# Strided slice on one core: a held batch moved from 128 partitions to 32 partitions with four rows each

## Chip, core and metric

The kernel runs on one core of one Trainium2 chip. The metric is device time in microseconds of one execution; lower is better.

## What is computed

```python
def reference(x, start, stop, stride):        # x: [32, 1024, 512] float32
    return x[:, start:stop:stride, :]         # start 0, stop 512, stride 2
```

Of each of the 32 batches every second row of the first 512 is copied: 256 rows of 512 float32 values (2 KB). The result is [32, 256, 512], 16.8 MB. There is no arithmetic, so the whole kernel is a set of DMA transfers. In `x` two chosen rows that follow each other start 4 KB apart and a batch starts 2 MB after the one before it. In `out` rows start 2 KB apart and batches 512 KB apart.

## The kernel before

The rows of a batch are parted by parity: 128 even output rows and 128 odd ones. One half is copied directly, from `x` to `out` in HBM. The other half takes a way through SBUF: it is loaded into the tile `held` and stored from there. `apart(b)` says which parity of batch b goes directly (1 for b = 0, 1, 4, 5 of eight, 0 for b = 2, 3, 6, 7). `two(t, b, step, parity)` makes the access pattern of one parity of the two batches b and b + step, with the 128 rows as its first dimension, the two batches as its second and the 512 values as its third. In `x` the 128 rows of one parity are 8 KB apart, in `out` 4 KB.

The batches are taken in four groups of eight (`EIGHT`). In the first double loop (lines 35 to 40) SP issues four loads in each group, each of two batches that follow each other (line 39), and ACT issues four direct copies, of the pairs (0, 5), (2, 7), (1, 4) and (3, 6) of the group (line 40). `held` is [128, 32, 512]: partition p holds row p of the loaded parity, for all 32 batches. Each transfer is 512 KB and moves rows of 2 KB.

In the second double loop (lines 41 to 47) both queues wait for the loads of a group, which count on a semaphore of their own in the list `loaded`, and then store it: four stores, each of batches b and b + 4, SP taking even b and ACT odd b (line 47). Each queue issues its instructions in the order of the program. ACT comes to its stores once it has issued all direct copies, SP once it has issued all loads. At the end SP waits for all stores and direct copies (lines 48 and 49), by the semaphores `done`. The tile is as large as all that is loaded, so no buffer is used twice.

The order is written out by hand; no scheduler moves a transfer.

Of the kernel before, what the change touches and what calls it, by code (L numbers as in the profile page):

```python
# [3 lines left out]

EIGHT = 8


def apart(b):


    return 1 - (b >> 1 & 1)


def two(t, b, step, parity):

    return t[b : b + step + 1 : step].rearrange("b (p two) d -> two p b d", two=2)[parity]


def kernel(tc, x, start, stop, stride, out):

    nc = tc.nc
    src = x[:, start:stop:stride, :]
    B, rows, D = out.shape
    P = rows // 2
    sp, act = nc.sync, nc.scalar
    groups = range(0, B, EIGHT)
    with tc.tile_pool(name="io", bufs=1) as io:  # L30
        held = io.tile([P, B, D], x.dtype, name="held")
        with tc.tile_critical():
            loaded = [nc.alloc_semaphore(name=f"loaded{g}") for g in groups]
            done = [nc.alloc_semaphore(name=f"done{i}") for i in range(2)]
            for g in groups:
                for i, (b, step) in enumerate(((0, 5), (2, 5), (1, 3), (3, 3))):
                    b += g
                    at = g + 2 * i
                    sp.dma_start(held[:, at : at + 2], two(src, at, 1, 1 - apart(at))).then_inc(loaded[g // EIGHT], 16)
                    act.dma_start(two(out, b, step, apart(b)), two(src, b, step, apart(b))).then_inc(done[1], 16)  # L40
            for g in groups:
                for queue in (sp, act):
                    queue.wait_ge(loaded[g // EIGHT], 16 * 4)
                for b in range(g, g + 4):
                    k = b % 2
                    to = two(out, b, 4, 1 - apart(b))
                    (sp, act)[k].dma_start(to, held[:, b : b + 5 : 4]).then_inc(done[k], 16)
            sp.wait_ge(done[0], 16 * (B // 4))
            sp.wait_ge(done[1], 16 * (B // 2 + B // 4))


# [1 line left out]
_INS = ['x', 'start', 'stop', 'stride']  # L53
_OUTS = [((32, 256, 512), 'float32')]

_NUMBERS = {'start': 0, 'stop': 512, 'stride': 2}


def kernel(**inputs):
    import numpy as _np  # L60
    import concourse.bacc as _bacc
    import concourse.tile as _tile
    from concourse import mybir as _mybir
    from concourse.bass_utils import run_bass_kernel_spmd as _run

    nc = _bacc.Bacc("TRN2", target_bir_lowering=False, num_devices=1)  # L66
    arrays, args = {}, []
    for name in _INS:
        if name in _NUMBERS:
            args.append(_NUMBERS[name])  # L70
            continue
        a = _np.ascontiguousarray(inputs[name])
        if a.dtype.kind in "iu":
            a = a.astype(_np.int64)
        arrays[f"in_{name}_dram"] = a
        args.append(nc.dram_tensor(f"in_{name}_dram", a.shape, _mybir.dt.from_np(a.dtype), kind="ExternalInput").ap())
    for i, (shape, dtype) in enumerate(_OUTS):
        dt = _mybir.dt.from_np(_np.dtype(dtype))
        args.append(nc.dram_tensor(f"out_{i}_dram", shape, dt, kind="ExternalOutput").ap())
    with _tile.TileContext(nc) as tc:  # L80
        kernel(tc, *args)
    r = _run(nc, [arrays], core_ids=[0])
    got = tuple(r.results[0][f"out_{i}_dram"] for i in range(len(_OUTS)))
    return got[0]
```

## Time and profile before

| | |
|---|---|
| median of 13 runs | 80.67 us (80.23 to 81.87) |
| the profiled execution's own time | 81.33 us |
| its span in the profile | 79.5 us |
| packets on the DMA engines | 13,056, of which 12,288 carry 2 KB and 768 signal completion |
| mean rate of the DMA engines over the span | 316 GB/s |
| loads (line 39) | 16 of 512 KB, median 22.6 us from issue to landing |
| direct copies (line 40) | 16 of 512 KB, median 22.6 us |
| stores (line 47) | 8 on SP and 8 on ACT, of 512 KB, median 20.9 and 20.7 us |

The span is the time from the first to the last recorded instruction; the execution's own time has some 1.8 us around it. GB/s counts what the 16 DMA engines of the core carried: a row that goes directly counts once, a row that goes through `held` counts twice, so that 16.8 MB of result are 25.2 MB of transfers. Queue q1 is SP's and q10 is ACT's. Both queues run on the same 16 engines. Time from issue to landing includes the wait behind what was issued before on the same queue.

The page's tables by compute engine hold nothing but four small fills by GpSimd at the start. Besides the page, the trace answers with a table by stretch of time (rate and busy share of the DMA engines), and it holds a record of every packet with its start, duration, queue and size.

### The profile page before, as it was taken

The page shows a single profiled execution, that of the slowest core. Times are in us where ns is not written, and L with a number is a line of the kernel's source. Part 1 is how long each engine was busy: PE and PEld are TensorE (multiplying, and loading weights), DVE is VectorE, ACT ScalarE, POOL GpSimd, SP SyncE. Part 2 cuts the span into 40 slices and gives each one's busy share as a digit, 9 for nine tenths or more (in the row PEclk, how much of TensorE's full clock was granted, in tenths as well). Part 3 has the DMA queues.
Part 4 walks back from the last instruction along what each step waited for, and adds up shares of the span by engine and source line. Part 5 has one row for each costly group of instructions (what it writes and reads, how often), then busy time and mean ns, then how long its engine had stood idle before and what let it go on. Part 6 is the DMA issues. An engine that isn't in the chain of part 4 may idle for free. (4 is left out here: it accounts for less than half of the span.)

```text
span 79.5 us, 99 instructions
## 1 busy us (share of the span) xinstructions
POOL 0.2 (0%) x4
## 2 busy tenths in 40 slices
POOL 0000000000000000000000000000000000000000
DMA  0899999999999999899999999999999999999930
GB/s 0 262 309 284 278 222 363 358 362 382 325 317 367 241 319 397 294 336 357 332 357 352 323 372 272 345 357 409 408 409 356 351 350 350 355 356 354 350 118 4
DMA packets 13056, 25.17 MB, mean 316 GB/s; under 512 B 768, under 2 KB 768, under 8 KB 13056
## 3 DMA queue, kind: packets, MB, share of 16 engines
q10 hardware_dynamic: 6528, 12.58, 47.6%
q1 hardware_dynamic: 6528, 12.58, 47.6%
HBM read 16.78 MB, written 16.78 MB: 422 GB/s over the span
## 5 line engine op out<-in xcount | busy, mean ns | idle before, releaser
L66 POOL MEMSET const-bfloat16-1.0<- 128x1 bf16 x1 | 0.1, 101 | 0.0
L66 POOL MEMSET const-uint8-127<- 128x1 uint8 x1 | 0.1, 101 | 0.0
L66 POOL MEMSET const-float32-0.0<- 128x1 f32 x1 | 0.1, 98 | 0.2 <-issue 0.2
L66 POOL MEMSET const-float32-1.0<- 128x1 f32 x1 | 0.1, 98 | 0.0
## 6 DMA issues: line engine op xcount, KB each, us to landing
out_dram<-in_x_dram ACTq DMA_DIRECT2D x16, 512.0 KB, 22.6
held<-in_x_dram SPq DMA_DIRECT2D x16, 512.0 KB, 22.6
out_dram<-held SPq DMA_DIRECT2D x8, 512.0 KB, 20.9
out_dram<-held ACTq DMA_DIRECT2D x8, 512.0 KB, 20.7
```

Of the source, the lines that this page charges most:

```text
L66: nc = _bacc.Bacc("TRN2", target_bir_lowering=False, num_devices=1)
```

## The change

A batch is now held by 32 partitions, with four rows in each. `held` becomes [128, 8, 4, 512]: batch b lies in the quarter b % 4 of the partitions, 32 x (b % 4) and on, at place b // 4. Its size stays the same, 64 KB in each partition. `place(b, n)` gives the part of the tile that holds n batches, and `pieces(t, b, n, parity)` the rows of one parity of n batches as [32 n, 4, 512].

- A load is of one batch, 256 KB, into 32 partitions; there are 32 instead of 16, in the order 0, 2, 1, 3, 4, 6, 5, 7 in each group, so that quarters 0 and 2 are followed by 1 and 3. A partition takes four rows, which are 8 KB apart in `x`.
- A store is of batches b and b + 1, from 64 partitions, 512 KB. SP stores those with b = 0 and 4 of the group, from partitions 0 to 63, ACT those with b = 2 and 6, from partitions 64 to 127. There are still 8 on each queue.
- A group's semaphore counts eight loads instead of four.
- The direct copies are the same, and stand in the same places on ACT.

In the built program the loads' pattern in `x` is 128 rows 8 KB apart, and the stores' in `out` 256 rows 4 KB apart; the SBUF side is 32 or 64 partitions of four rows of 2 KB. If the 16 engines take runs of equal length of these rows, an engine's part begins 64 KB after its neighbour's, in `x` for loads and in `out` for stores.

```diff
+QUARTER = 32
+DEEP = 4
...
+def pieces(t, b, n, parity):
+
+    rows = t[b] if n == 1 else t[b : b + n].rearrange("b r d -> (b r) d")
+    return rows.rearrange("(p s two) d -> two p s d", s=DEEP, two=2)[parity]
...
-    P = rows // 2
...
-        held = io.tile([P, B, D], x.dtype, name="held")
+        held = io.tile([4 * QUARTER, B // 4, DEEP, D], x.dtype, name="held")
+
+        def place(b, n):
+            first = QUARTER * (b % 4)
+            return held[first : first + n * QUARTER, b // 4]
...
                 for i, (b, step) in enumerate(((0, 5), (2, 5), (1, 3), (3, 3))):
+                    for at in ((0, 2), (1, 3), (4, 6), (5, 7))[i]:
+                        at += g
+                        sp.dma_start(place(at, 1), pieces(src, at, 1, 1 - apart(at))).then_inc(loaded[g // EIGHT], 16)
                     b += g
-                    at = g + 2 * i
-                    sp.dma_start(held[:, at : at + 2], two(src, at, 1, 1 - apart(at))).then_inc(loaded[g // EIGHT], 16)
                     act.dma_start(two(out, b, step, apart(b)), two(src, b, step, apart(b))).then_inc(done[1], 16)
             for g in groups:
                 for queue in (sp, act):
-                    queue.wait_ge(loaded[g // EIGHT], 16 * 4)
-                for b in range(g, g + 4):
-                    k = b % 2
-                    to = two(out, b, 4, 1 - apart(b))
-                    (sp, act)[k].dma_start(to, held[:, b : b + 5 : 4]).then_inc(done[k], 16)
+                    queue.wait_ge(loaded[g // EIGHT], 16 * EIGHT)
+                for b in range(g, g + EIGHT, 2):
+                    k = b // 2 % 2
+                    (sp, act)[k].dma_start(pieces(out, b, 2, 1 - apart(b)), place(b, 2)).then_inc(done[k], 16)
```

## The prediction

> **What bounds the kernel now.** I read the page's slices and queue table first, then the table by stretch of time, then the issue table and the wait list. No compute engine does anything, so the time is that of 12,288 packets of 2 KB on 16 DMA engines, 768 each.
>
> ```profile
> span 79.5 us, 99 instructions
> DMA  0899999999999999899999999999999999999930
> q10 hardware_dynamic: 6528, 12.58, 47.6%
> q1 hardware_dynamic: 6528, 12.58, 47.6%
> HBM read 16.78 MB, written 16.78 MB: 422 GB/s over the span
> ```
>
> The reader is to see that the DMA engines are busy from the second slice to the last but two, and that the queues of SP and ACT get equal shares. A packet sooner is a gain only if it takes an engine less long. How long it takes shows in the rate by stretch:
>
> ```profile
> core 0: us, POOL busy (x), PEclk, DMA share, GB/s
> 2.00:56.00 54.00, 0.00 (x0) 1.00 1.00 330
> 54.00:55.00 1.00, 0.00 (x0) 1.00 1.06 408
> 56.00:57.00 1.00, 0.00 (x0) 1.00 1.06 410
> 56.00:76.00 20.00, 0.00 (x0) 1.00 1.06 361
> 68.00:70.00 2.00, 0.00 (x0) 1.00 1.07 353
> 76.00:79.50 3.50, 0.00 (x0) 1.00 0.10 36
> ```
>
> The last number of a row is GB/s. 16 x 2048 bytes over it is an engine's pace per packet: 99.3 ns up to 56 us, where loads and direct copies run (stage one), 90.8 ns from 56 to 76 us, where stores run (stage two), and 80.3 ns at 54 to 55 us, the best seen. 768 packets at 80.3 ns would be 61.7 us; they took from 2.0 to 77.9 us. The 14 us between: stage one 330 x 54 us = 17.8 MB = 544 packets an engine x 19.0 ns = 10.3 us; stage two 220 packets x 10.5 ns = 2.3 us; a tail from 76 us on, in which few engines still work, some 1.5 us. The trace's packet records tell the nature of the loss: most packets take exactly 84 ns (the next starts 4 ns before the end). In stage one some 316 took over 200 ns, many of them ending within some 50 ns of others, and hold nearly all the excess; in stage two none did, but from 59 us on about half take 86 to 200 ns.
>
> Issue and semaphores are not the limit:
>
> ```profile
> out_dram<-in_x_dram ACTq DMA_DIRECT2D x16, 512.0 KB, 22.6
> held<-in_x_dram SPq DMA_DIRECT2D x16, 512.0 KB, 22.6
> SPq L49 <- DMA out_dram<-held: 19.5, 1, 19.5
> SPq L47 <- DMA held<-in_x_dram: 0.5, 1, 0.5
> ```
>
> A DMA lands 22.6 us after its issue, so the rings hold over 20 us of work, and the one wait of 0.5 us for loads (line 47) hides behind them. SP then waits 19.5 us for stores only at the end.
>
> **What the Trainium skill says.** "DMA: Bandwidth & Descriptors", section "The descriptor swizzle": a transfer over 128 partitions gives engines 0 to 7 partitions 4e to 4e+3 and 32+4e to 35+4e, engines 8 to 15 the upper half. Neighbouring engines of a load would then read x 4 x 8 KB = 32 KB apart, those of a store write 4 x 4 KB = 16 KB apart, each engine with a port of its own. Its section "Why a DMA increments its semaphore by 16 and not by 1" lets 32 or 64 partitions still use 16 engines, since 16 divides both; which engine gets which rows it does not say, and I assume runs of equal length. "SBUF — State Buffer", section "Door 1: The DMA port swizzle", says that partitions 0 to 31 or 0 to 63 reach only 8 of 16 ports, 189 to 196 GB/s at 1 MiB against an asymptote of 218 (27.2 a port). No stretch of this trace shows such a shape. "Latency and other measured facts" on the first page gives copies between HBM tensors 207 GB/s at a row pitch of 512 KB and 214 at best, and less only at pitches of 2 MB and more; the trace can't confirm or deny it, as it varies no pitch.
>
> **The change part by part.**
>
> *16 loads of 512 KB become 32 of 256 KB.* Packets stay 2 KB and 4,096. Each engine has 16 completion packets more, at 9 ns in the packet records: 0.15 us. That they cost more at a boundary is excluded by 53 to 59 us, where completions pass and the rate stays at 399 to 410. SP issues 16 DMAs more, at 433 ns (the least for a load) to 652 ns (the least on ACT) each, 7 to 10 us in all; that runs under the backlog of 20 us and costs nothing except at the start. Two loads go with one direct copy, 1.05 MB or 3.2 us at 330 GB/s; SP needs some 1.9 us for them at 0.94 us each, the longest that an ACT issue took in the first 2 us. Over 1.6 us each the cover would be gone.
>
> *Start.* The first load may be issued in 652 instead of 433 ns: 0 to 0.2 us. Loads run alone from 2.0 to 3.6 us, at some 246 GB/s by the slices of that stretch; over 8 ports at 189 to 218 that is 1.6 us x (1 - 189/246) = 0.4 us at most, 0.2 at least. I take 0.4 for both.
>
> *Loads over 32 partitions.* Two neighbouring engines now share a port. On average the loads bring 330/2 = 165 GB/s, under 189, so a port isn't full. But a load packet can find its partner at work: the port needs 2048/27.2 = 75 ns, the partner puts one there every 199 ns, so 38% of packets wait 37 ns on average, 14 ns x 256 packets = 3.6 us for random phases with no read-ahead; nothing if the pairs fall into opposite phase, which alternating with direct copies permits. I take a sixth, 0.6 us[...].
>
> *Stores over 64 partitions.* SP's stores read partitions 0 to 63, ACT's 64 to 127, so each queue has 8 ports and engines e and e+8 share one. At 361/2 = 180 GB/s a queue stands close to 189. By the same sum: partner every 182 ns, 41% x 37 ns x 256 = 3.9 us at random, 0 at best; I take a sixth, 0.65 us. Where one queue works alone, as at 75 to 76 us where most packets are ACT's, another 0.1 us.
>
> *Distance of the engines, 64 KB in x and in out.* This is the part that the trace does not show, so it is bounded on both sides. For it: load packets stall more often than direct ones (194 against 122 over 200 ns from 2 to 56 us). Against it: the mean of both is 99.2 ns there, and from 20 to 56 us the direct ones, which stand at 64 KB in x already, are the slower. Stalls that end together hit direct copies too, six engines at a time for 1.2 to 1.5 us. For loads all excess gone is (99.2 - 84) x 256 = -3.9 us; a worsening as large is not excluded, +3.9. For stores: -2.3 us (408 GB/s held to the end) to (99.3 - 90.8) x 220 = +1.9 us, if they take on stage one's pace. I take 0 for both.
>
> *Waits and order.* `loaded` counts 128 instead of 64; a group of loads ends at the same byte. Stores take b and b+1 together, needing the same group, and SP and ACT still have 8 each. Behind SP's waits stand only its stores, with 20 us queued ahead. Cost nothing, on that cover.
>
> Sum: 0.15 + 0.4 + 0.6 + 0.65 + 0.1 = +1.9 us. The profiled execution took 81.33 us, 1.8 us around its span of 79.5, so 83.2 us by its own time; it lay 0.66 us above the median of 80.67 us, against which I forecast **82.6 us**.
>
> **Rivals.**
> 1. *Likeliest, 0.40: shared ports nibble, distance does nothing.* 82.6 us, its own range 81 to 84.
> 2. *Slower by more, 0.15: paired engines stay in step,* two thirds of the port waits count: 2.4 + 2.6 + 0.65 = +5.6 us, 86.3. For it: all engines get equal DMAs at once, and stage two has 5 to 21% of room to the port limit (180 against 189 to 218). Against: at the best pace every packet is 84 ns, so engines drift only by stalls, and opposite phase is stable.
> 3. *Faster, 0.39: the distance cures stalls.* One mechanism, 16 streams meeting in one part of HBM. With half of the loads' excess gone (-1.95) and stores at 385 GB/s instead of 361 (-1.25), against 0.65 for start, completions and tail: -2.5 us, 78.1 us. It decides once it saves more than 1.9 us, that is 7.4 ns on each load packet alone. For it: groups of load stalls ending together, and the fall from 408 to 353 GB/s among stores, which neither queue nor port explains. Against: direct copies with that distance are no better.
> 4. *The change doesn't do what it says, or gains and costs cancel, 0.06:* the rows are dealt to engines otherwise, distances stay mixed; 80.7 us.
>
> **How the numbers follow.** Slower is cases 1 and 2, 0.55; faster 0.39; within 0.3% (0.24 us, about what a measurement of this kernel can tell from no change) 0.06. The range 78.0 to 86.2 us takes in case 1, nearly all of case 2 up to its centre, and case 3 down to its centre.
>
> **What would show it.** Right: over the first 54 us the rate stays at 320 to 335 GB/s with as many packets over 200 ns in loads as now; stage two falls to 340 to 352; the 408 GB/s stretch at the turn of the stages gets shorter or lower; the first 2 us of transfer are slower. Wrong: stage one at 345 or more, or stage two near 400, says the distance matters and ports don't; a rate per queue that never passes 190 with packets at 100 ns and more throughout says case 2. A longer gap before the first packet would be issue cost that I put at 0.2 us.

## The result, and the profile after

The changed kernel takes 82.12 us (median of 11 runs, 81.65 to 82.57) against 80.62 us before (48 runs): ratio 1.0175, 95% interval 1.0144 to 1.0206. It is slower by 1.4 to 1.5 us; the forecast was 82.6 us. The sign and the size came out, but the experiments below show that most of the terms of the sum were put in the wrong place.

The two profiled executions lie nearer to each other than the medians: 81.33 us before (0.7 above its median) and 81.72 after (0.4 below). So the profiles show how the two kernels differ in kind, and less than the whole difference in size: their last packets end 0.5 us apart. The page after:

```profile
span 79.9 us, 115 instructions
DMA  0799899999999999999999999999999999999730
q1 hardware_dynamic: 6784, 12.59, 47.2%
q10 hardware_dynamic: 6528, 12.58, 45.8%
HBM read 16.78 MB, written 16.78 MB: 420 GB/s over the span
```

The queue of SP (q1) has 256 packets more than before: 16 loads more, each with 16 completions. Its share of engine time is no larger (47.2% of 79.9 us against 47.6% of 79.5), so a packet did not get dearer on average; ACT's share even fell, from 47.6% to 45.8%. The same stretches as in the prediction, after:

```profile
core 0: us, POOL busy (x), PEclk, DMA share, GB/s
2.00:56.00 54.00, 0.00 (x0) 1.00 0.99 328
56.00:57.00 1.00, 0.00 (x0) 1.00 1.03 399
56.00:76.00 20.00, 0.00 (x0) 1.00 1.02 359
68.00:70.00 2.00, 0.00 (x0) 1.00 1.06 353
76.00:79.90 3.90, 0.00 (x0) 1.00 0.17 67
```

Stage one moves at 328 GB/s (330 before), stage two at 359 (361), and its settled part at 353 in both. What differs is the last row: 67 GB/s over 3.9 us, where before had 36 over 3.5. Neither the loads nor the stores got slower as a whole; the end got longer. A finer table shows it. (The changed kernel's 362 GB/s from 60 to 73 us, below, still holds a part of the fast stretch at the turn of the stages, which comes later in it.) Before:

```profile
60.00:73.00 13.00, 0.00 (x0) 1.00 1.06 353
73.00:75.00 2.00, 0.00 (x0) 1.00 1.07 348
75.00:76.00 1.00, 0.00 (x0) 1.00 0.98 322
76.00:77.00 1.00, 0.00 (x0) 1.00 0.29 102
77.00:79.00 2.00, 0.00 (x0) 1.00 0.03 11
```

After:

```profile
60.00:73.00 13.00, 0.00 (x0) 1.00 1.06 362
73.00:75.00 2.00, 0.00 (x0) 1.00 0.88 311
75.00:76.00 1.00, 0.00 (x0) 1.00 0.60 231
76.00:77.00 1.00, 0.00 (x0) 1.00 0.43 166
77.00:79.00 2.00, 0.00 (x0) 1.00 0.13 48
```

GB/s times us gives what is left at 73 us: 348 x 2 + 322 + 102 + 22 = 1,142 KB before, 311 x 2 + 231 + 166 + 96 = 1,115 KB after. So at 73 us the changed kernel is not behind. But before keeps its engines busy to nearly 76 us (share 1.07, 0.98), and all but one of them then stop within about a microsecond, while after has idle engines from 73 us on (0.88, 0.60, 0.43) and works until 78.4 us. Taken that each engine gets an equal part of every transfer, as the prediction did, the engines run out of equal lists of packets at different times. The packet records, put into chains by their start and end over the last microseconds, give it by engine. This is approximate, to some tenths of a microsecond, since a record doesn't name its engine. Before, 15 of 16 end between 75.7 and 76.8 us and one at 77.9; after, eight end between 76.0 and 78.4 us and eight between some 73 and 75.5. The mean of the 16 is about 76.3 us before and 76.0 after. The time of the kernel is that of its last engine.

The issues and waits, after:

```profile
out_dram<-in_x_dram ACTq DMA_DIRECT2D x16, 512.0 KB, 20.8
held<-in_x_dram SPq DMA_DIRECT2D x32, 256.0 KB, 16.3
SPq L62 <- DMA out_dram<-held: 11.6, 1, 11.6
SPq L60 <- DMA held<-in_x_dram: 0.3, 1, 0.3
```

A load lands 16.3 us after its issue, so once the queues are filled the doubled number of issues hides behind the backlog, as forecast, and the wait for loads is 0.3 us.

### The profile page after: what moved, and what is told of

Same layout as the page of the kernel before. It is cut to its first block, busy times and chain, and to the rows that moved or that the text cites. A ratio compares the mean times of both kernels' runs of the same rounds, so it can differ in the third digit from the quotient of the medians.

```text
span 79.9 us, 115 instructions
## 1 busy us (share of the span) xinstructions
POOL 0.2 (0%) x4
## 3 DMA queue, kind: packets, MB, share of 16 engines
q1 hardware_dynamic: 6784, 12.59, 47.2%
q10 hardware_dynamic: 6528, 12.58, 45.8%
## 6 DMA issues: line engine op xcount, KB each, us to landing
held<-in_x_dram SPq DMA_DIRECT2D x32, 256.0 KB, 16.3
```

## The experiments

The theories at the outset: P, ports shared by two engines cost a little on every packet (the forecast's own); E, the two ends of the kernel (SP's loads begin at 3.9 us instead of 2.0 in the packet records, and SP ends alone); D, the distance between engines. Each kernel has the time of the kernel before measured beside it on its chip, and a ratio below is against that time. The excerpts leave out the lines that count the semaphores, where only the number of transfers changes in them.

**The loads alone, and the stores alone.** `flat` is `held` seen as [128, 32, 512].

```diff
 # e_loads: the changed kernel with the stores of before
-                for b in range(g, g + EIGHT, 2):
-                    ...place(b, 2)
+                for b in range(g, g + 4):
+                    ...flat[:, b : b + 5 : 4]
 # e_stores: the changed kernel with the loads of before
-                    for at in ((0, 2), (1, 3), (4, 6), (5, 7))[i]: ...
+                    sp.dma_start(flat[:, at : at + 2], two(src, at, 1, 1 - apart(at)))...
```

> Only the loads are changed (32 of 256 KB into 32 partitions); the stores are those of before, 128 partitions, batches b and b + 4. Each store reads the group's data in the old places, so rows come out permuted within a group of eight. Before 80.6 us, after 82.1. Theory P (shared ports cost a little on every packet, in both stages): half of the loss, 81.2 us. Theory E (the loss lies at the two ends: SP's queue starts 1.9 us later than before, falls behind ACT's, and ends alone with stores that reach 8 ports): the start is lost and the end is not, 81.0 to 81.4 us, with SP's last packets at 16 ports faster than in the changed kernel. Theory D (the distance between engines matters): no fixed value, but stage one differs from before by over 1 us.

> Only the stores are changed (64 partitions, batches b and b + 1); the loads are those of before, 128 partitions. Rows come out permuted within a group of eight. Theory P: the other half, 81.4 us, with the rate between 60 and 75 us below 350 GB/s. Theory E: the start is that of before (first packet of SP at 2.0 us), ACT ends last by about 1 us as before, now on 8 ports: 80.6 to 81.2 us. Theory D: stage two at 360 GB/s or more if 64 KB is better for stores, then under 80.4 us.

Measured: loads alone 1.0217 (1.0174 to 1.0260), stores alone 1.0021 (1.0000 to 1.0043). The loads carry the whole loss. Stores that read 64 partitions, b and b + 1, with engines 64 KB apart if they take equal runs, cost 0.2%, at most 0.4%. Theory P had asked for 81.4 us from the stores and got 80.84, so its second half is gone as a cost that matters, though its sign, a rate below 350 GB/s from 60 to 75 us, came narrowly (350 and 346, from 353 and 348). Gone too is a gain for stores by distance:

```profile
60.00:73.00 13.00, 0.00 (x0) 1.00 1.06 350
73.00:75.00 2.00, 0.00 (x0) 1.00 1.06 346
75.00:76.00 1.00, 0.00 (x0) 1.00 0.88 305
76.00:77.00 1.00, 0.00 (x0) 1.00 0.25 94
```

These last rows also have the sharp end of before (1.06, 0.88, 0.25): the long end comes with the loads. With the loads alone changed, the share falls to 0.63, 0.56 and 0.21 in the last three stretches. It shows long after the loads: in the changed kernel their last packets end at 56.4 us by the packet records, and the first engines stand idle at 73.

**The ports.**

```diff
         def place(b, n):
-            first = QUARTER * (b % 4)
-            return held[first : first + n * QUARTER, b // 4]
+            step = 4 // n
+            return held[b % 4 // n :: step, b // 4]
```

> The changed kernel with its partitions spread: a load goes to every fourth partition, a store reads every second one, so that each transfer touches all 16 ports of the Trainium skill's port map, while sizes, counts and HBM addresses of the transfers stay. Stores read other rows than belong there (permuted within a group). Theory P: the port share goes, 80.9 us. Theory E: only the lone end gets faster, 81.3 to 81.8 us. Theory D, or ports that never mattered: 82.1 us.

Measured: 1.0204 (1.0155 to 1.0253), as the changed kernel. Giving each transfer all 16 ports of the map brings nothing back. That fits what the Trainium skill says in "SBUF — State Buffer", section "Door 1: The DMA port swizzle": 8 ports carry 189 to 196 GB/s at 1 MiB, and the loads, at half of 328 GB/s, need 164. No run here shows the limit; the most that came over 8 ports is 191 GB/s, by the packet records of SP's stores in the changed kernel from 60 to 73 us.

**The distance.**

```diff
-    pieces: rows.rearrange("(p s two) d -> two p s d", s=DEEP, two=2)[parity]
+    loads:  t[b].rearrange("(s p two) d -> two p s d", s=DEEP, two=2)[parity]
```

> The changed kernel with only the rows of a load dealt otherwise: partition p takes rows p, 32 + p, 64 + p and 96 + p of the parity, so that neighbouring engines read 16 KB apart in x instead of 64 KB, with the same partitions, sizes and counts. Rows come out permuted within a batch. Theories P and E: 82.1 us as the changed kernel. Theory D: it differs from 82.1 by over 0.5 us, upwards if 64 KB helps, downwards if it hurts.

Measured: 1.0239 (1.0193 to 1.0285), again as the changed kernel within the intervals. If the engines take equal runs, 16 KB or 64 KB between neighbours is the same. The edit also moves an engine's own successive rows apart, from 8 to mostly 256 KB, so the two could in principle cancel. This kernel starts like before, with SP's first packet at 1.96 us, so theory E's start is not the cause either. Its end is the plainest of all:

```profile
2.00:56.00 54.00, 0.00 (x0) 1.00 1.00 331
73.00:75.00 2.00, 0.00 (x0) 1.00 0.80 289
75.00:76.00 1.00, 0.00 (x0) 1.00 0.48 184
76.00:77.00 1.00, 0.00 (x0) 1.00 0.36 141
77.00:79.00 2.00, 0.00 (x0) 1.00 0.13 50
79.00:81.00 2.00, 0.00 (x0) 1.00 0.02 8
```

It moved as much in the first 56 us as before (331 GB/s) and had less left at 73 us, 1,019 KB, but needed until 79.7 us for it. (The profiled execution is the slowest of its six, 82.93 us against a median of 82.44.)

**The kernel before with its loads split by batch.** With ports, distance and start gone, what is left of the loads is their number and their shape.

```diff
-                    at = g + 2 * i
-                    sp.dma_start(held[:, at : at + 2], two(src, at, 1, 1 - apart(at)))...
+                    for at in (g + 2 * i, g + 2 * i + 1):
+                        sp.dma_start(held[:, at], one(src, at, 1 - apart(at)))...
```

> The kernel before with each load split in two: 32 loads of 256 KB, of one batch each, into all 128 partitions; nothing else. So far: only the loads of the change cost time, and neither the ports nor the distance of the engines do. Theory N (the number of load transfers: 16 more completions for each engine, one batch in flight at a time): as the loads alone, 82.2 us. Theory M (the shape over 32 partitions, whose rows are dealt to the engines otherwise than those of 128): as before, 80.7 us.

Measured: 1.0146 (1.0094 to 1.0198). Still 128 partitions, still the old rows in the old partitions, and most of the loss is there. The shape over 32 partitions is not needed for it. Its end is long as well:

```profile
75.00:76.00 1.00, 0.00 (x0) 1.00 0.75 291
76.00:77.00 1.00, 0.00 (x0) 1.00 0.52 201
77.00:79.00 2.00, 0.00 (x0) 1.00 0.16 62
```

**One group of eight in the old form.**

```diff
+ if g == 0:             # e_last_old: if g == B - EIGHT
+     the loads and stores of before
+ else:
      the loads and stores of the changed kernel
```

> The changed kernel with the first group of eight (loads and stores) in the old form, the other three in the new. Theory of the start (SP's queue begins 1.9 us late and never catches up): the loss is gone, 80.8 us, with SP's first packet at 2.0 us. Theory that each load in the new form costs alike: three quarters of the loss stay, 81.7 to 81.9 us.

> The changed kernel with the last group of eight in the old form, the other three in the new. Theory of the start: no gain, 82.2 us. Theory that each new load costs alike: 81.7 to 81.9 us. Theory of the end (the last stores over 64 partitions, drained by one queue alone): the loss is mostly gone, 81.0 us.

Measured: 1.0305 (1.0258 to 1.0352) and 1.0300 (1.0249 to 1.0352). All three theories missed: a kernel that mixes the forms is slower than either. With the first group old, SP's first packet is at 2.05 us and both queues are level at 53 us (3,944 and 3,966 packets of 2 KB), and the kernel is slow all the same. But whatever a cured start or end gains could hide under the cost of the mixture, so these two runs don't settle where the loss lies. They also show that the loss doesn't go with the number of new loads: 24 of them with 4 old ones cost more than 32. Why the mixture costs more was not found.

**Number or batches: four kernels on one chip.** First the changed kernel again:

> The changed kernel once more, for a comparison on one chip with the three others: 1.5 to 2.2% over before, by all theories. Engines are expected to finish over more than 3 us in it (8 of 16 at 76 to 78.4 us, the others at 74.0 to 75.6 in the first profile, by the packet records), where before had 15 of 16 within 1 us.

Measured: 1.0190 (1.0149 to 1.0231). By the packet chains its engines end from some 73 to 79.5 us.

Then the loads of before split by partitions instead of by batch: as many loads as in the changed kernel, 256 KB each, but two batches in each.

```diff
                     at = g + 2 * i
-                    sp.dma_start(held[:, at : at + 2], two(src, at, 1, ...))
+                    for first in (0, 64):
+                        sp.dma_start(held[first : first + 64, at : at + 2], two(src, at, 1, ...)[first : first + 64])
```

> The kernel before with each load split by partitions: 32 loads of 256 KB, each of two batches into 64 partitions; the stores and the rest are those of before. Theory N1 (the number of load transfers alone costs): 1.3 to 2% over before. Theory N2 (what costs is that a load holds one batch, so that an engine reads eight neighbouring rows in a row and not two batches in turn): as before, within 0.4%.

Measured: 0.9992 (0.9971 to 1.0014). The loss is gone, with 32 loads, 32 sets of completions, 64 partitions at a time (8 ports by the map), SP's first packet at 3.8 us, and SP behind ACT by 524 packets of 2 KB at 53 us (514 in the changed kernel). SP also ends alone here: its last packet comes 2.8 us after ACT's, against 2.7 in the changed kernel. Number, ports, start, lag and the lone end of theory E are all in this kernel and cost nothing together. The end is short again:

```profile
73.00:75.00 2.00, 0.00 (x0) 1.00 1.03 346
75.00:76.00 1.00, 0.00 (x0) 1.00 0.57 205
76.00:77.00 1.00, 0.00 (x0) 1.00 0.22 86
77.00:79.00 2.00, 0.00 (x0) 1.00 0.00 0
```

Third, the direct copies split by batch, with the loads of before:

```diff
-                    act.dma_start(two(out, b, step, apart(b)), two(src, b, step, apart(b)))...
+                    for at in (b, b + step):
+                        act.dma_start(one(out, at, apart(at)), one(src, at, apart(at)))...
```

> The kernel before with each direct copy split in two: 32 direct copies of one batch and 256 KB each; the loads and stores are those of before. Theory N1, if any transfer more costs alike: 1.3 to 2% over before. If only loads do: as before. Theory N2 for HBM rows in general: slower here too, since a direct copy then holds one batch as well.

Measured: 1.0150 (1.0111 to 1.0190). A transfer of one batch costs on the other queue as well, whose copies have no SBUF side. Its end is long:

```profile
73.00:75.00 2.00, 0.00 (x0) 1.00 0.74 278
75.00:76.00 1.00, 0.00 (x0) 1.00 0.47 182
76.00:77.00 1.00, 0.00 (x0) 1.00 0.31 121
77.00:79.00 2.00, 0.00 (x0) 1.00 0.16 60
```

The last two tables are the comparison to keep. At 73 us both kernels have the same left (983 and 979 KB) and both have 32 transfers on one queue; the one with two batches in each ends its packets at 77.0 us, the one with one batch at 79.0 us. (The two profiled executions, 80.43 and 82.33 us, lie 1.9 us apart; the medians, 80.67 and 81.73, lie 1.1 apart.)

Fourth, fewer and larger loads, of four batches:

```diff
-                    at = g + 2 * i
-                    sp.dma_start(held[:, at : at + 2], two(src, at, 1, ...))
+                    if g % 16 == 0:
+                        at = g + i
+                        sp.dma_start(held[:, at : at + 13 : 4], four(src, at, ...))
```

> The kernel before with 8 loads of 1 MB instead of 16 of 512 KB: each of four batches, b, b + 4, b + 8 and b + 12, into 128 partitions; the stores of sixteen batches wait for four such loads. Theory N1: fewer transfers, so faster than before, by up to 0.8%. Theory N2 (batches in turn are what is needed): as before. If a load of 1 MB holds back the end of the loads and with it the first stores, slower by 0.5% or more.

Measured: 1.1969 (1.1927 to 1.2011). No theory had 20%. Fewer loads are no gain here, and something new costs far more. Part of it may be a wait: SP stands 8.7 us for loads before its stores, against 0.5 us before. But the transfers themselves are slow too, 257 GB/s from 2 to 56 us instead of 330.

**Which batches are taken in turn.** The four batches of that kernel are 8 MB apart in `x`. The last run puts that distance into the kernel before, with the size and number of the loads left as they were.

```diff
-                    at = g + 2 * i
-                    sp.dma_start(held[:, at : at + 2], two(src, at, 1, 1 - apart(at)))...
+                    at = g + i
+                    sp.dma_start(held[:, at : at + 5 : 4], two(src, at, 4, 1 - apart(at)))...
```

> The kernel before with other pairs in its loads: batches b and b + 4 (8 MB apart in x) instead of b and b + 1 (2 MB apart); sizes, counts, partitions and all else as before. Theory that the eight loads of 1 MB cost 20% by the place in x that an engine's packets alternate between: slower by over 4%, with loads' packets of 110 ns and more. Theory that they cost it by their size and the late stores: as before, within 0.5%.

Measured: 1.0586 (1.0529 to 1.0643). Pairs 8 MB apart cost 5.9% against pairs 2 MB apart. Besides the distance only the order changed in which the batches of a group are loaded, and so which batches the two queues read at one time; a share of that isn't excluded. Stage one itself is slower here, 310 GB/s from 2 to 56 us instead of 330; by the packet records a packet of SP's queue takes 108.5 ns on average up to 56 us (99.2 before), and 290 of them over 200 ns (194). And the end is longer still:

```profile
75.00:76.00 1.00, 0.00 (x0) 1.00 0.78 301
77.00:79.00 2.00, 0.00 (x0) 1.00 0.57 219
79.00:83.00 4.00, 0.00 (x0) 1.00 0.23 89
```

Distance alone doesn't explain it: the direct copies of the kernel before take pairs 6 and 10 MB apart in `x`, and their packets average 99.2 ns from 2 to 56 us, as its loads do, though no run tried 6 or 10 MB for loads. The Trainium skill, "DMA: Bandwidth & Descriptors", section "Latency and other measured facts", has copies between HBM tensors slow down at row pitches of 2 MB and more, to half at 4 and 8 MB. The direction agrees at 8 MB. But the page's pitch lies between the rows of neighbouring partitions, and here neighbouring rows are 8 KB apart and 8 MB is the step between the two places that one load takes in turn, so this is a likeness and no test of the page. At 2 MB nothing of the kind shows here: loads that take two batches 2 MB apart in turn do better than loads of one batch (0.9992 against 1.0146).

## Why the prediction was right or wrong

- *The sum and the sign.* +1.9 us forecast, +1.4 to 1.5 measured. The likeliest case, "shared ports nibble, distance does nothing", gave the right number, and its second half held as far as it was tested. That the number came out is luck: the ports and the start, 1.75 of the 1.9 us, measure at next to nothing, and what does cost is not in the sum.
- *Distance of the engines, taken as 0: right as far as tested.* 16 KB instead of 64 KB for loads, by equal runs, changes 1.0190 to 1.0239, with intervals that overlap; for stores the change to 64 KB is 1.0021. The argument that carried it was that the direct copies already stood at 64 KB and were no better. The bounds of 3.9 us on either side were far too wide.
- *Ports, +0.6 for loads, +0.65 and 0.1 for stores: wrong.* Stores over 64 partitions cost 0.2%, 0.17 us, with an interval down to none; loads over 64 partitions with two batches cost nothing; spreading the changed kernel over 16 ports brings nothing back. The step that failed is taking a sixth of a random collision without any evidence that a collision stops an engine; the 75 ns for which a packet holds a port was itself an estimate from the 27.2 GB/s a port that the prediction cites, and no run shows it. The sign the prediction asked for, settled stage two at 340 to 352 GB/s and a lower peak, did not come: 353 at 68 to 70 us in both. Nor did the fast stretch at the turn of the stages get shorter. It got longer, as the page's slices of 2 us show, before and after:

```profile
GB/s 0 262 309 284 278 222 363 358 362 382 325 317 367 241 319 397 294 336 357 332 357 352 323 372 272 345 357 409 408 409 356 351 350 350 355 356 354 350 118 4
GB/s 0 224 158 320 289 371 290 355 371 285 349 337 335 362 310 325 343 338 339 324 341 347 340 338 303 353 401 405 410 409 406 369 351 351 354 350 334 272 125 12
```

Three slices over 400 became five. (The best pace in the prediction's own table is 410 GB/s at 56 us, not the 408 at 54 that it takes; nothing hangs on it.)

- *Start, +0.4: seen, but not where time is lost.* The rate from 2 to 5 us fell from 277 to 214 GB/s. SP's first packet came 1.9 us later, where 0.2 us at most had been put down, while ACT's came 1.2 us earlier. The kernel of 64 partitions and two batches has the same late packet and 239 GB/s there, and loses nothing by the end.
- *"16 loads become 32, packets stay": this term was mis-sized.* It was put at 0.15 us of completions, with more excluded. The completions are indeed free (0.9992 with 32 loads). But the step overlooked that each load also went from two batches to one. Loads of one batch in 128 partitions cost 1.46%, 1.2 us, most of the loss, and they cost it some 17 us after the loads, at the end, as engines that run dry at different times. The prediction had seen the tail, 1.5 us "in which few engines still work", and took it as given; it is the quantity that the change moved.
- *Issue, waits and order, at nothing: right.* 16.3 us from issue to landing, 0.3 us of wait.
- *The faster rival* needed long stalls to go. They stayed: 188 of SP's packets over 200 ns from 2 to 56 us, 194 before. The rival of engines in step had settled rates falling, and they did not.

What stays open: why engines get further apart when each transfer holds one batch. The runs show that it happens with loads and with direct copies, with 32 partitions and with 128, and not with 32 loads of two batches. It doesn't grow with the number of one-batch loads, since 24 of them beside 4 old ones cost 3%, and two batches don't cure it at 8 MB. The stores may say more: in the changed ones all rows of a partition lie in one batch of `out`, and they cost 0.2%. If the engines take equal runs, that points to the reading from one batch and not to the writing; no run was made for this. That an engine's next packet then lies 8 KB from the last, and not 2 MB, is one reading, which the kernel with a partition's rows 256 KB apart only narrows: steps of 256 KB within one batch do not cure it (1.0239); that certain places in HBM are slower for certain engines was not tried, since a record does not name its engine. The kernel split by batch (1.0146) and the changed one (1.0190 and 1.0175) overlap in their intervals, so whether the 32 partitions add anything is open too. No version here beats the kernel before clearly.

## What to carry to other kernels

When a kernel is nothing but DMA, look at how its engines run out, not only at how fast they run: a mean rate that is the same to 1% can hide an end in which the engines stop over some 5 us instead of 2, and the share of busy engines in the last 5 us shows it. When a transfer is cut in two, ask along which dimension: cut by partitions it cost nothing here, cut by batch 1.5%. Which far places a transfer takes in turn is worth its own experiment: 2 MB against 8 MB was 5.9%, more than anything that was tried on ports and on the distance between engines.

## What was not expected of the hardware

- 8 ports did not show: transfers over 64 partitions, at 165 GB/s (loads, 20 to 56 us) to 176 GB/s (stores, 60 to 73 us) for a queue by the packet records, beside another queue, cost nothing for the loads (0.9992) and 0 to 0.4% for the stores.
- A pattern 8 MB apart is costly even between just two batches (5.9%). With four it was 19.7%, in which the larger loads and the wait for them may have their part.
- A change in the loads, whose packets end at 56.4 us, can show in hardly any rate until the last 5 us (328 against 330 GB/s from 2 to 56 us). There engines stand idle for microseconds (share 0.43 from 76 to 77 us) while others still have packets, so no work passed from one to another.
